# The reciprocal root of each norm: nine small VectorE operations where there were twelve

## The chip, the cores and the metric

The kernel runs on one core of one Trainium2 chip. The metric is device time in microseconds for one launch of the whole layer. A profiled execution also gives a trace of every instruction on the core's engines: TensorE (PE; its weight loads are listed apart as PEld), VectorE (DVE), ScalarE (ACT), GpSimd (POOL), and the queue from which transfers are issued (SP).

## The reference

One layer of a decoder on 1024 tokens of width 1024, in float32. Five kinds of norm run through it, and the change touches nothing else.

```python
def rms_norm(x, gain):
    xf = x.astype(jnp.float32)
    y = xf * lax.rsqrt(jnp.mean(xf * xf, axis=-1, keepdims=True) + EPS)
    return (y * gain.astype(jnp.float32)).astype(x.dtype)
...
    h = modulate(rms_norm(x, ffn1_norm[l]), sh1, sc1)
    x = x + 0.5 * g1[:, None, :] * swiglu(h, ...)              # width 2816
    h = modulate(rms_norm(x, mix_norm[l]), sh2, sc2)
    b_gate, c_gate, v, u = jnp.split(h @ w_in[l], ...)
    y_conv = short_conv_mixer(b_gate, c_gate, v, conv_w[l])
    y_ssm = s5_mixer(u, ...)                                  # diagonal state space, then a GLU
    y_mix = jnp.concatenate([rms_norm(y_conv, out_norm_conv[l]),
                             rms_norm(y_ssm, out_norm_ssm[l])], axis=-1)
    x = x + g2[:, None, :] * (y_mix @ w_out[l])
    h = modulate(rms_norm(x, ffn2_norm[l]), sh3, sc3)
    x = x + 0.5 * g3[:, None, :] * swiglu(h, ...)
return rms_norm(x, final_norm)
```

The nine vectors of shift, scale and gate come from a product of `silu(cond)` with a matrix of 1024 by 9216.

## The kernel before, in words

Activations lie transposed: the 128 partitions hold channels, the columns hold tokens. The 1024 tokens are two halves of 512 (`h` = 0, 1), the 1024 channels are eight tiles (`k`). Each large product is made of three matmuls with a high and a low part of both operands (`mm3`). ScalarE copies the high part of a weight tile and VectorE subtracts it for the low part; in the trace these are the rows that write `w`.

The stages follow each other: a prologue with the first norm (`p`); the first feed-forward block (names with `fa`, down projections `fad` and `fald`); the norm `n2`; the input projection (`u`, `c`, `v`, `b`) with the state space; the output norms `nA` (convolution) and `nB` (state space); the GLU (`gl`, whose input is split into `yg`); the output projection (`wo`); the norm `n3`; the second feed-forward block (`fb`, last products `fb10d`); the final norm in pieces, `n_0` for the first 512 tokens, `n_0` again for 256 and `n_256` for the last 256. A trailing `a` or `b` in a name is the half of the tokens. Products of the modulation matrix (`wm`), one for each 128 by 1024 piece of it, run on VectorE beside the main work, each after its own transfer into one of two buffers.

A norm goes like this (class `Sumsq`). ScalarE squares the tiles, VectorE or GpSimd add them, and small matmuls with a column of ones (`st`) put the sums of 128 tokens at a time into one column: 512 tokens become a block of 128 by 4. `roots` computes the reciprocal root of this block on VectorE, `wide` repeats each of the four columns 128 times (`rb`), and `spread` turns the result by matmuls with the identity, so that every partition holds the root of every token (`bc`). The consumers multiply by it.

The operations of `roots` write four small tiles: `v` (the mean plus epsilon), `i` (its bits as an integer), `a` and `y`; in the trace a norm's name, an `n` and that letter, as in `nBana`. Twelve norms of the program run `roots`: p, with 8 columns, two widenings and two `bc`; n2a, n2b, nAa, nAb, nBa, nBb, n3a, n3b and the first n_0, with 4; the second n_0 and n_256, with 2.

In the program, matmuls drive a counter (`Clock`): after each `mm3` it ticks, and `rstd` puts the sums, the root and the spreading some ticks later, so that matmuls of other work stand between them. Where a consumer needs the result at once, the counter is run forward (`ready`, `clock.until`), and nothing stands between. The order in which the instructions then stand on each engine is made by a planner of the framework, from dependencies, the order of the program and free buffers. Only in the prologue is the order of each engine fixed to that of the program:

```python
    InOrder.strict = True
    ...
    InOrder.strict = False
```

Almost every engine call goes through the helper `InOrder`, so the profile puts nearly all instructions at line 107, and groups are told apart by the tiles they write and read.

Of the kernel before, what the change touches and what calls it, by code (L numbers as in the profile page):

```python
# [15 lines left out]
I32 = mybir.dt.int32  # L16
AF = mybir.ActivationFunctionType
ALU = mybir.AluOpType
# [3 lines left out]
P = 128  # L22
# [30 lines left out]
RC2 = float(np.float32(np.round((TWO_PI - RC1) * 2.0**20) / 2.0**20))  # L53
RC3 = float(np.float32(TWO_PI - RC1 - RC2))
ROUND = 12582912.0
EXP_C = [1.9875691500e-4, 1.3981999507e-3, 8.3334519073e-3, 4.1665795894e-2, 1.6666665459e-1, 5.0000001201e-1]


# [173 lines left out]
def hymba_layer(ctx: ExitStack, tc, x_d, wm1_d, wmod_d, gu1_d, gs1_d, ds1_d, wl1_d, win_d, wout_d, glu_d, gu2_d, gs2_d, wd2_d, ds2_d, wl2_d, cols_d, cond_d, lam_d, bc_d, out_d):  # L232
    nc = tc.nc
    V, A, T, SP = (InOrder(tc, e) for e in (nc.vector, nc.scalar, nc.tensor, nc.sync))
# [33 lines left out]
    def t2k(name):  # L268
        return tmp.tile([P, HALF], F32, tag="t", name=name)
# [82 lines left out]
    class Sumsq:  # L352
# [28 lines left out]
        def rstd(self, width, use, wait=4, wait2=7):  # L381
            q = self.n // P

            def stats():
                st = sm([P, 4], self.name + "st")
                self.sums(st)
                y = roots(st, q, width, self.name)
                rb = wide(y, self.name)
                clock.after(wait2, lambda: use(spread(rb, self.name)))

            clock.after(wait, stats)

    def roots(st, q, width, nm):

        v, y, a = (const.tile([P, 8], F32, tag=f"n{i}", name=f"{nm}n{i}", bufs=1)[:, :q] for i in "vya")
        yi = const.tile([P, 8], I32, tag="ni", name=nm + "ni", bufs=1)[:, :q]
        V.tensor_scalar(out=v, in0=st[:, :q], scalar1=1.0 / width, scalar2=EPS, op0=ALU.mult, op1=ALU.add)
        V.tensor_scalar(out=yi, in0=v.bitcast(I32), scalar1=1, scalar2=None, op0=ALU.logical_shift_right)
        V.tensor_scalar(out=yi, in0=yi, scalar1=-1.0, scalar2=1597463007.0, op0=ALU.mult, op1=ALU.add)
        src = yi.bitcast(F32)  # L400
        for _ in range(3):
            V.tensor_tensor(out=a, in0=src, in1=src, op=ALU.mult)
            V.scalar_tensor_tensor(out=a, in0=a, scalar=-0.5, in1=v, op0=ALU.mult, op1=ALU.mult)
            V.scalar_tensor_tensor(out=y, in0=a, scalar=1.5, in1=src, op0=ALU.add, op1=ALU.mult)
            src = y
        return y

    def wide(y, nm):
        q = y.shape[1]
        rb = t2k(nm + "rb")[:, : q * P].rearrange("p (a b) -> p a b", a=q)  # L410
        V.tensor_copy(rb, y.unsqueeze(2).to_broadcast([P, q, P]))
        return rb

    def spread(rb, nm):
# [358 lines left out]
    for h in range(2):  # L773
# [7 lines left out]
        q = sqs[0]  # L781
        V.tensor_tensor(out=q[:, :HALF], in0=q[:, :HALF], in1=q[:, HALF:], op=ALU.add)
        for i in range(4):
            c = 4 * h + i
            T.matmul(st[:, c : c + 1], lhsT=q[:, i * P : (i + 1) * P], rhs=one[:], start=True, stop=True)
    y = roots(st, 8, D, "p")
    rbs = [wide(y[:, 4 * h : 4 * h + 4], f"p{h}") for h in range(2)]
    ws.open(ringp, 2)
    w4 = ws.take(2)
# [94 lines left out]
    def ssm_base(sb1):  # L884
# [9 lines left out]
        def exp_(dst, src):  # L894
            k, r, z, s = w[0], w[1], w[2], w[3]
            V.tensor_scalar(out=s, in0=src, scalar1=-87.0, scalar2=88.0, op0=ALU.max, op1=ALU.min)
            V.tensor_scalar(out=k, in0=s, scalar1=1.0 / math.log(2.0), scalar2=ROUND, op0=ALU.mult, op1=ALU.add)
            V.tensor_scalar(out=k, in0=k, scalar1=ROUND, scalar2=None, op0=ALU.subtract)
            V.scalar_tensor_tensor(out=r, in0=k, scalar=-0.693359375, in1=s, op0=ALU.mult, op1=ALU.add)
            V.scalar_tensor_tensor(out=r, in0=k, scalar=2.12194440e-4, in1=r, op0=ALU.mult, op1=ALU.add)  # L900
            V.tensor_scalar(out=z, in0=r, scalar1=EXP_C[0], scalar2=None, op0=ALU.mult)
            for c in EXP_C[1:]:
                V.scalar_tensor_tensor(out=z, in0=z, scalar=c, in1=r, op0=ALU.add, op1=ALU.mult)
            V.tensor_tensor(out=z, in0=z, in1=r, op=ALU.mult)
            V.scalar_tensor_tensor(out=z, in0=z, scalar=1.0, in1=r, op0=ALU.add, op1=ALU.add)
            ki = sb1.tile([P, G], I32, tag="ki", name="ki", bufs=2)
            V.tensor_scalar(out=ki[:], in0=k, scalar1=127.0, scalar2=8388608.0, op0=ALU.add, op1=ALU.mult)
            V.tensor_tensor(out=dst, in0=z, in1=ki[:].bitcast(F32), op=ALU.mult)
# [7 lines left out]
        exp_(r, ar)  # L916
        V.tensor_scalar(out=w[0], in0=th, scalar1=1.0 / TWO_PI, scalar2=ROUND, op0=ALU.mult, op1=ALU.add)
        V.tensor_scalar(out=w[0], in0=w[0], scalar1=ROUND, scalar2=None, op0=ALU.subtract)
        for c in (RC1, RC2, RC3):
# [747 lines left out]
```

## Time and profile before

| | |
|---|---|
| median of three runs | 1745.43 us (1743.46 to 1748.77) |
| profiled execution: time | 1741.48 us |
| its span, first to last instruction | 1739.7 us |
| TensorE busy | 1672.0 us, 96% |
| VectorE busy | 1291.1 us, 74%, 2261 instructions |
| ScalarE busy | 573.3 us, 33% |
| GpSimd busy | 352.8 us, 20% |
| mean granted TensorE clock | 0.992 |

Busy time is summed over stages with different limits. A row of a timeline gives the start, the duration, the engine, the operation, the tiles written and read, the shapes and the number of instructions merged in the row; in brackets stands how long the engine was idle before it and which instruction ended that. A row of the windows gives a stretch, its length, the busy time with the number of instructions, the granted clock, the share of the transfer engines and GB/s. A row of the groups gives the number of instructions, their busy time in us, the mean of one in ns and the idle time before them.

### The profile page before, as it was taken

Reading aid. Unit: us, or ns where it says so; the run is one execution under the profiler, and the core shown is the slowest. Engines: PE = TensorE matmul, PEld = TensorE weight load, DVE = VectorE, ACT = ScalarE, POOL = GpSimd, SP = SyncE. Lnnn points to the kernel's source line nnn. Section 1 sums busy time; section 2 is a strip of 40 time slices with the busy share of each in tenths; the row PEclk is TensorE's granted clock in tenths of the full one; section 3 lists DMA queues with packets and bytes.
Section 4 is the critical chain, followed back from the end, with each engine's and each line's share of the span. In section 5 each row is a group of like instructions: output and inputs, shape, how many; then the busy total and the mean of one; then the engine's idle time right before and its main releaser. Section 6 shows DMA issues by size and latency. Waiting matters only on the chain.

```text
span 1739.7 us, 20839 instructions
## 1 busy us (share of the span) xinstructions
PE 1672.0 (96%) x7532; PEld 1375.3 (79%) x7532; DVE 1291.1 (74%) x2261; ACT 573.3 (33%) x944; POOL 352.8 (20%) x241
## 2 busy tenths in 40 slices
PE   4999999999999999999999999999999999999996
PEld 3788888787887878887877778778888888888886
DVE  7999999998656787644657977967776666576656
ACT  4233334344332222331114424424444433322221
POOL 0000132222422221100000021123223323333211
PEclk9999999999999999999999999999999999999998
DMA  8245644555787877234654450114344334659212
GB/s 322 84 145 197 220 158 167 179 201 173 286 307 275 321 259 270 73 86 147 209 152 152 134 181 25 49 49 157 144 175 166 133 138 152 249 235 379 104 49 97
DMA packets 101338, 304.56 MB, mean 175 GB/s; under 512 B 19313, under 2 KB 34929, under 8 KB 90098
## 3 DMA queue, kind: packets, MB, share of 16 engines
q1 hardware_dynamic: 101234, 303.22, 49.0%
q8 instruction: 59, 0.97, 0.2%
q14 instruction: 45, 0.37, 0.1%
HBM read 212.47 MB, written 86.51 MB: 172 GB/s over the span
## 4 chain that ended last, share of the span: by engine, by line
PE 64%; DVE 8%; DMA 3%; issue 1%; ACT 0%; POOL 0%; SPq 0%; DVEq 0%; ACTq 0%; POOLq 0%
PE wo L107 4%; PE fald L107 3%; PE fb10d L107 2%; PE u L107 2%; PE fbd_1B L107 2%; PE fbd_0B L107 2%; PE fad_1B L107 2%; DVE w L107 2%; PE fad_0B L107 2%; PE b L107 2%; DMA swz<-si 1%; DVE x L107 1%; PE fb0g L107 1%; PE fbd_1C L107 1%; PE fbd_0C L107 1%; PE fbd_1A L107 1%
## 5 line engine op out<-in xcount | busy, mean ns | idle before, releaser
L107 ACT CAST w<-raw 128x512 fp32r<-128x512 f32 (+1 forms) x358 | 235.9, 689 | 459.1 <-issue 70.1
L107 DVE TENSOR_TENSOR w<-raw,w 128x512 fp32r<-128x512 f32 (+1 forms) x358 | 300.9, 860 | 100.8 <-ACT w L107 99.9
L164 POOL TENSOR_TENSOR sums<-raw 128x512 f32<-128x512 f32 x50 | 73.8, 1476 | 452.9 <-DMA raw<-in_gs 271.0
L173 POOL TENSOR_TENSOR raw<-sums,raw 128x512 f32<-128x512 f32 x50 | 78.4, 1568 | 367.3 <-DVE w L107 353.7
L107 DVE CUSTOM_DVE_ANT_0 wm<-wm,cact 128x1024 f32<-128x1024 f32 x56 | 77.7, 1396 | 22.6 <-DMA wm<-in_wmod 22.6
L175 POOL TENSOR_TENSOR raw<-raw 128x512 f32<-128x512 f32 x50 | 77.1, 1542 | 79.1 <-DVE w L107 79.1
L165 POOL TENSOR_TENSOR raw<-raw 128x512 f32<-128x512 f32 x50 | 77.3, 1547 | 3.1
L366 POOL TENSOR_TENSOR n3aq<-n3aq,n3aq 128x512 f32<-128x512 f32 x5 | 7.4, 1474 | 279.1 <-ACT n3aq L107 278.9
L107 DVE TENSOR_TENSOR w<-sums,w 128x512 fp32r<-128x512 f32 x50 | 56.7, 1147 | 5.4 <-ACT w L107 4.8
L107 PE MATMUL p<-h,w 128*128 128x512 f32 x192 | 49.6, 421 | 8.1 <-DVE h L107 5.3
L107 PEld LDWEIGHTS p<-h,w 128*128 128x128 f32 x192 | 39.1, 205 | 18.6 <-DVE h L107 6.5
L107 PE MATMUL wo<-oa,w 128*128 128x512 f32 x192 | 45.6, 392 | 2.1 <-ACT w L107 1.4
L107 PE MATMUL v<-h,w 128*128 128x512 f32 x192 | 46.8, 395 | 0.0
L107 PE MATMUL c<-h,w 128*128 128x512 f32 x192 | 46.6, 394 | 0.0
L107 PE MATMUL b<-h,w 128*128 128x512 f32 x192 | 45.6, 393 | 0.0
L107 PE MATMUL wo<-ob,w 128*128 128x512 f32 x192 | 45.5, 392 | 0.0
L107 PE MATMUL u<-h,w 128*128 128x512 f32 x192 | 44.7, 391 | 0.2 <-DVE h L107 0.2
L107 PEld LDWEIGHTS wo<-oa,w 128*128 128x128 f32 x192 | 35.8, 188 | 10.2 <-ACT w L107 1.8
L107 PEld LDWEIGHTS u<-h,w 128*128 128x128 f32 x192 | 35.7, 188 | 8.3 <-DVE h L107 0.6
L107 PEld LDWEIGHTS wo<-ob,w 128*128 128x128 f32 x192 | 35.7, 188 | 7.7 <-DVE ob L107 0.4
L107 PEld LDWEIGHTS b<-h,w 128*128 128x128 f32 x192 | 35.5, 188 | 7.2
L107 PEld LDWEIGHTS c<-h,w 128*128 128x128 f32 x192 | 35.4, 188 | 7.0
(1566 smaller groups left out, 4028.4 us busy)
## 6 DMA issues: line engine op xcount, KB each, us to landing
raw<-in_gs SPq DMA_DIRECT2D x34, 1024.0 KB, 5.5
wm<-in_wmod SPq DMA_DIRECT2D x56, 512.0 KB, 5.8
raw<-in_ds SPq DMA_DIRECT2D x16, 1024.0 KB, 6.8
raw<-in_gu SPq DMA_DIRECT2D x10, 1024.0 KB, 7.1
mw<-in_wm SPq DMA_DIRECT2D x8, 1024.0 KB, 12.4
x<-in_x SPq DMA_DIRECT2D x16, 512.0 KB, 8.3
raw<-in_win SPq DMA_DIRECT2D x8, 1024.0 KB, 5.6
raw<-in_wl SPq DMA_DIRECT2D x5, 1024.0 KB, 6.6
```

The lines of the kernel that those rows point to most:

```text
L107: r = getattr(self.engine, name)(*args, **kw)
L164: self.G.tensor_tensor(out=f, in0=r[2], in1=r[1], op=ALU.subtract)
L165: self.G.tensor_tensor(out=r[1], in0=r[1], in1=r[0], op=ALU.subtract)
L173: self.G.tensor_tensor(out=r, in0=s["t3"], in1=r, op=ALU.add)
L175: self.G.tensor_tensor(out=r, in0=self.chunk(j, 3), in1=r, op=ALU.subtract)
L366: nc.gpsimd.tensor_tensor(out=a, in0=a, in1=sq[:, :n], op=ALU.add)
```

## The change

The seed of the root is the usual one from the bits of the float: half of the bits, subtracted from a constant. Before, one operation shifts the bits and a second negates and adds. After, one operation multiplies the integer by −0.5 and adds a constant. Then, before, three Newton steps of three operations each. After, one step with tuned constants in three operations, and a step of third order in four. That step ends with a factor of 0.375, which is left out of the root; the widening, a copy before, multiplies by it. In all, nine operations in place of twelve, and no other edit.

```diff
+ROOT_BITS, ROOT_A, ROOT_B = 1595932665.0, 0.703952253, 2.38924456
...
         V.tensor_scalar(out=v, in0=st[:, :q], scalar1=1.0 / width, scalar2=EPS, op0=ALU.mult, op1=ALU.add)
-        V.tensor_scalar(out=yi, in0=v.bitcast(I32), scalar1=1, scalar2=None, op0=ALU.logical_shift_right)
-        V.tensor_scalar(out=yi, in0=yi, scalar1=-1.0, scalar2=1597463007.0, op0=ALU.mult, op1=ALU.add)
+        V.tensor_scalar(out=yi, in0=v.bitcast(I32), scalar1=-0.5, scalar2=ROOT_BITS, op0=ALU.mult, op1=ALU.add)
         src = yi.bitcast(F32)
-        for _ in range(3):
-            V.tensor_tensor(out=a, in0=src, in1=src, op=ALU.mult)
-            V.scalar_tensor_tensor(out=a, in0=a, scalar=-0.5, in1=v, op0=ALU.mult, op1=ALU.mult)
-            V.scalar_tensor_tensor(out=y, in0=a, scalar=1.5, in1=src, op0=ALU.add, op1=ALU.mult)
-            src = y
+        V.scalar_tensor_tensor(out=a, in0=src, scalar=-ROOT_A, in1=src, op0=ALU.mult, op1=ALU.mult)
+        V.tensor_tensor(out=a, in0=a, in1=v, op=ALU.mult)
+        V.scalar_tensor_tensor(out=y, in0=a, scalar=ROOT_A * ROOT_B, in1=src, op0=ALU.add, op1=ALU.mult)
+        V.tensor_tensor(out=a, in0=y, in1=y, op=ALU.mult)
+        V.tensor_tensor(out=a, in0=a, in1=v, op=ALU.mult)
+        V.scalar_tensor_tensor(out=a, in0=a, scalar=-10.0 / 3.0, in1=a, op0=ALU.add, op1=ALU.mult)
+        V.scalar_tensor_tensor(out=y, in0=a, scalar=5.0, in1=y, op0=ALU.add, op1=ALU.mult)
         return y
...
-        V.tensor_copy(rb, y.unsqueeze(2).to_broadcast([P, q, P]))
+        V.tensor_scalar(out=rb, in0=y.unsqueeze(2).to_broadcast([P, q, P]), scalar1=0.375, scalar2=None, op0=ALU.mult)
```

## Prediction

> **What bounds the kernel now.** I read the page first, for the busiest engine and for the chain that ended last.
>
> ```profile
> span 1739.7 us, 20839 instructions
> PE 1672.0 (96%) x7532; PEld 1375.3 (79%) x7532; DVE 1291.1 (74%) x2261; ACT 573.3 (33%) x944; POOL 352.8 (20%) x241
> PE 64%; DVE 8%; DMA 3%; issue 1%; ACT 0%; POOL 0%; SPq 0%; DVEq 0%; ACTq 0%; POOLq 0%
> ```
>
> TensorE is busy for 96% of the span, and the chain lies on it for 64%; VectorE (DVE) holds only 8% of the chain. A shorter norm on DVE can therefore bring time only where TensorE stands still for it. So the second view is the waits of TensorE: who waited for whom, microseconds in total, times, longest.
>
> ```profile
> PE n_256bc L107 <- DVE n_256rb L107: 4.2, 1, 4.2
> PE nBabc L107 <- DVE nBarb L107: 3.9, 1, 3.9
> PE p0bc L107 <- DVE p0rb L107: 3.0, 1, 3.0
> PE n_0bc L107 <- DVE n_0rb L107: 2.5, 1, 2.5
> PE gl L107 <- DVE yg L107: 1.9, 1, 1.9
> PE nAbbc L107 <- DVE nAbrb L107: 1.7, 1, 1.7
> ```
>
> Each norm ends in `rb`, the widened root, and `bc`, eight (or four) matmuls that spread it. Twelve norms run `roots`, and only five of them (p, nAb, nBa, the second n_0, n_256) stand here; `gl`, behind `yg`, is a neighbour of nAb. 17.2 us in all is the most that norms could ever give back.
>
> **The change part by part.** *The three operations removed.* `roots` issues twelve small operations before and nine after: 36 fewer in twelve norms. The price of one is read where they run back to back, in the prologue (timeline of VectorE, start and duration; then TensorE).
>
> ```profile
> 22.11 0.17 DVE L107 TENSOR_SCALAR pnv<-p_st 128x8 f32<-128x8 f32 x1 [1.96 <-PE p_st L107]
> 24.53 0.43 DVE L107 COPY p0rb<-pny 128x512 f32<-128x512 f32 x1
> 25.10 2.05 PE L107 MATMUL p0bc<-ident,p0rb 128*128 128x128 f32 x8 [3.03 <-DVE p0rb L107]
> ```
>
> Twelve operations lie between 22.11 and 24.53: 2.42/12 = 0.202 us each, start to start, of which 0.17 is the operation. Three fewer are 0.61 us. The new operations are of the removed kinds at the same width, and I price them alike; the fused bit step takes the place of a multiply-add on the same integers.
>
> [...]
>
> *The prologue.* There the order of issue is tied down, TensorE waits 3.0 us for `p0rb`, and everything after starts from it: −0.61 us, which the rest of the kernel inherits.
>
> *Norms that TensorE does not wait for.* In the main part the spreading matmuls come some 20 matmuls after the sums, and those cover the root:
>
> ```profile
> 719.03 0.43 DVE L107 COPY n2arb<-n2any 128x512 f32<-128x512 f32 x1
> 720.36 1.05 PE L107 MATMUL n2abc<-ident,n2arb 128*128 128x128 f32 x8
> ```
>
> `n2arb` ends 0.9 us before TensorE comes to it. The bc of n2b, n3a, n3b, nAa, nBb and the first n_0 are not in the list of waits either: 0 for these seven. Were the matmuls in front gone, their roots would show in full (0.6 us of saving each); nothing in the change touches them.
>
> *nAb.* Here two waits must be kept apart.
>
> ```profile
> 940.88 0.16 DVE L107 TENSOR_SCALAR nAbnv<-nAbst 128x4 f32<-128x4 f32 x1 [1.15 <-PE nAbst L107]
> 943.06 0.69 DVE L107 TENSOR_TENSOR yg<-yb,yg 128x512 fp32r<-128x512 f32 x1 [0.23 <-issue]
> 943.86 0.16 DVE L107 SCALAR_TENSOR_TENSOR nAbny<-nAbna,nAbny 128x4 f32<-128x4 f32 x1
> 952.64 0.42 DVE L107 COPY nAbrb<-nAbny 128x512 f32<-128x512 f32 x1
> ```
>
> The root is done at 944.0 and the widening runs at 952.64: the wait of 1.7 us at `nAbbc` is not the root's, 0 from it. But `yg`, for which `gl` waits, stands behind ten of the root's operations. If it goes behind seven, −0.6; if the planner puts nine and the widening ahead of it, +0.2. I take −0.4.
>
> *nBa.*
>
> ```profile
> 967.45 1.23 DVE L107 TENSOR_TENSOR w<-raw,w 128x1024 fp32r<-128x1024 f32 x1 [0.86 <-ACT w L107]
> 971.06 1.22 DVE L107 CUSTOM_DVE_ANT_0 wm<-wm,cact 128x1024 f32<-128x1024 f32 x1
> 972.21 0.16 DVE L107 SCALAR_TENSOR_TENSOR nBany<-nBana,nBany 128x4 f32<-128x4 f32 x1
> 972.97 2.04 PE L107 MATMUL nBabc<-ident,nBarb 128*128 128x128 f32 x8 [3.92 <-DVE nBarb L107]
> ```
>
> Between `w`, which the root does not hold up, and `nBarb` lie the nine operations of the three old steps, and large ones of other work. Seven take the place of the nine; the third removed operation stood ahead of `w` and brings nothing. So −0.4, at 0.2 each. If the two stood inside other work they would be worth 0.08 each, −0.16; that is the near bound, and the far one is a rival below.
>
> *The end.* After the last weights the span is a chain on VectorE.
>
> ```profile
> 1720.64 0.16 DVE L107 TENSOR_SCALAR n_0ni<-n_0nv 128x2 int32<-128x2 int32 x1
> 1720.73 0.48 DVE L107 SCALAR_TENSOR_TENSOR x<-fb10d,gate,x 128x256 f32<-128x256 f32 x1
> 1725.74 0.29 DVE L107 COPY n_0rb<-n_0ny 128x256 f32<-128x256 f32 x1
> 1730.51 0.16 DVE L107 TENSOR_TENSOR n_256na<-n_256ny 128x2 f32<-128x2 f32 x1
> 1731.69 0.29 DVE L107 COPY n_256rb<-n_256ny 128x256 f32<-128x256 f32 x1
> 1733.30 3.22 DVE L107 SCALAR_TENSOR_TENSOR x<-x,cols,n_256bc 128x256 f32<-128x256 f32 x8 [1.32 <-PE n_256bc L107]
> ```
>
> The second n_0 runs in the gaps of output work: an operation between two large ones costs 0.09 (1720.64 to 1720.73), a free-standing one 0.2. Three fewer are −0.26 to −0.6; VectorE is full there and most stand in gaps, so −0.3. In n_256 the last six operations run alone (1.18/6 = 0.197 each) and the output multiplies follow: −0.59.
>
> *The widening.* A copy of 128x512 becomes a multiply by 0.375. The trace has no such multiply at 512 columns.
>
> ```profile
> L107 DVE TENSOR_SCALAR w<-w 128x32 f32<-128x32 f32 x18 | 3.2, 180 | 0.5
> L107 DVE TENSOR_SCALAR tab<-pw 64x288 f32<-64x288 f32 x4 | 1.2, 300 | 0.0
> L107 DVE TENSOR_TENSOR X<-X,st 128x512 f32<-128x512 f32 x8 | 5.5, 691 | 0.2
> ```
>
> The two TENSOR_SCALAR rows give 120 ns for 256 columns, so 405 ns at 512, against 0.43 us for the copy: nothing, or 0.02 gained. The other bound is a two-input operation, 691 ns: +0.26 in each of the two p widenings and nBa, +0.13 in each of the two half-width ones, about +1.1 us in all. I take 0, by the rows of its own kind.
>
> *Sum:* −0.61 −0.4 −0.4 −0.3 −0.59 = −2.3 us. The change adds no wait and no transfer, and moves no step past a queue. The profiled execution took 1741.48 us (its span is 1739.7) and would take 1739.2. It lies 4 us under the median of the three runs, 1745.43, which becomes 1743.1, or −0.13%. Less than 0.3%, 5.2 us, a measurement of this kernel can hardly tell from no change.
>
> **The rivals.** All rest on one thing that the trace shows: in the code a root's operations follow each other, but on VectorE other work stands between them. A planner orders the engines, and three fewer operations can change its order anywhere.
>
> *Faster, the waits shrink further.* If the second `wm` of nBa (1.15 us from 971.06 to 972.21) falls behind the widening, and `nAbrb` moves forward to its root, that is −1.15 and −1.7. Then TensorE's clock joins in.
>
> ```profile
> 972.90:974.70 1.80, 1.73 (x9) 0.50 0.64 180
> 953.10:954.10 1.00, 0.99 (x9) 1.00 0.85 324
> 953.11 1.16 PE L107 MATMUL nAbbc<-ident,nAbrb 128*128 128x128 f32 x8 [1.74 <-DVE nAbrb L107]
> 974.67 3.77 PE L107 MATMUL gl<-yg,w 128*128 128x512 f32 x12
> 936.62 2.88 PE L107 MATMUL gl<-yg,w 128*128 128x512 f32 x12
> ```
>
> After the wait of 3.92 us the granted clock was 0.50; after 1.74 us it was 1.00. The same eight matmuls took 2.04 against 1.16, and the twelve behind them 3.77 against 2.88: the drop cost 0.88 + 0.89 = 1.8 us. Together: 2.3 + 1.15 + 1.7 + 1.8 = 7.0, 1738.5 us. For it: the planner has moved such work through every root in sight, and `nAbrb` stands 8.6 us behind its root. Against it: three steps have to fall together.
>
> *The clock alone.* The wait falls from 3.9 to 3.5 us and the clock stays up: −2.3 − 1.8 = −4.1, 1741.3 us. The trace says only that the limit lies between 1.74 and 3.92 us, so 3.5 is more likely beyond it than not. [...]
>
> *It does less than it says.* Other work closes the gaps at nAb, nBa and n_0; the prologue and n_256 remain: −1.2, 1744.2 us.
>
> *Slower: a `wm` ahead of a weight.* `wm` are the side products that wait for their own loads.
>
> ```profile
> 1021.06 3.44 DVE L107 TENSOR_TENSOR w<-raw,w 128x1024 fp32r<-128x1024 f32 x2
> 1024.43 2.31 DVE L107 CUSTOM_DVE_ANT_0 wm<-wm,cact 128x1024 f32<-128x1024 f32 x1
> 1026.66 1.22 DVE L107 CUSTOM_DVE_ANT_0 wm<-wm,cact 128x1024 f32<-128x1024 f32 x1
> 1031.61 1.22 DVE L107 CUSTOM_DVE_ANT_0 wm<-wm,cact 128x1024 f32<-128x1024 f32 x1 [3.72 <-DMA wm<-in_wmod]
> ```
>
> If the planner lets the weights at 1021.06 slip behind these three, TensorE, which needs them at once, waits until 1032.8 minus 1024.4 = 8.4 us longer: 1745.43 − 2.3 + 8.4 = 1751.5 us. Two of them alone cost 3.4 and leave the time about as it was. It decides from the third on. For it: loads are late there (3.72 us). Against it: the planner held the weights first here.
>
> **How the numbers follow.** The forecast as summed 0.46 (its own range 1742.6 to 1745.1, all lower and all upper bounds of its terms added); the clock alone 0.16; less than it says 0.10; faster together 0.19; slower 0.09. Within 0.3% are the first three, 0.72; faster 0.19; slower 0.09. The range runs from just under the faster rival, 1737.0, to 1748.5, where two thirds of the slower one's price are paid; what is left out is the full slower case and a little of the faster.
>
> **What would show it.** Nine operations in each root of the changed profile, 36 fewer on VectorE and about 6 us less busy time; `p0bc` 0.6 us earlier; the wait of `n_256bc` 0.6 shorter, 3.6 us; `nBabc` waiting 3.5; the widening at 0.41 to 0.43 us; the granted clock at `nBabc`. It is wrong if VectorE's order differs around `wm`, `nAbrb` or the weights, or if the widening comes near 0.69 us.

## The result, and the profile after

The median fell from 1744.75 to 1741.66 us (17 runs of each; 1742.04 to 1748.77 before, 1735.41 to 1744.90 after). The ratio, worked out from all the runs, is 0.9974, with a 95% interval of 0.9966 to 0.9982: 4.5 us less, between 3.1 and 5.9; the two medians alone differ by 3.1. The forecast was 2.3 us less.

The profiled execution of the changed kernel took 1742.49 us, 1.0 more than the one of before. Single executions differ by the granted clock (0.988 to 0.993 in the 17 of the changed kernel, with 1735.41 to 1744.90 us), so that two spans alone decide nothing here. The cores view of the changed kernel gives the span and the mean granted clock (1739.7 us and 0.992 before).

```profile
core 0: 1740.3 us, clock 0.989
```

The clock's shortfall from 1, times the span, is an estimate of the most time given up: 1739.7 × 0.008 = 13.9 us and 1740.3 × 0.011 = 19.1 us. At the same clock the changed kernel's execution would by that be 0.6 − 5.2 = 4.6 us shorter, with about 1.2 us of rounding: the size of the ratio. What the change did must be read from its places, then. The page of the changed kernel:

```profile
PE 1674.2 (96%) x7532; PEld 1377.1 (79%) x7532; DVE 1287.5 (74%) x2225; ACT 573.8 (33%) x944; POOL 352.2 (20%) x241
```

VectorE has 36 operations fewer, as forecast, and 3.6 us less of busy time, not the 6 forecast, so 0.10 us for each: many stand between large operations and overlap them (in the trace of before, one of 0.16 us at 1720.64 and a large one 0.09 us later). One constant more in the file puts the helper at line 108. TensorE's waits for norms, of the changed kernel (total, times, longest):

```profile
PE n_256bc L108 <- DVE n_256rb L108: 3.8, 1, 3.8
PE p0bc L108 <- DVE p0rb L108: 2.4, 1, 2.4
PE nBabc L108 <- DVE nBarb L108: 2.3, 1, 2.3
PE n_0bc L108 <- DVE n_0rb L108: 1.9, 1, 1.9
PE nAbbc L108 <- DVE nAbrb L108: 1.7, 1, 1.7
PE gl L108 <- DVE yg L108: 1.7, 1, 1.7
PE nBbbc L108 <- DVE nBbrb L108: 0.7, 1, 0.7
```

Five fell: p from 3.0 to 2.4, the second n_0 from 2.5 to 1.9, n_256 from 4.2 to 3.8, `gl` behind `yg` from 1.9 to 1.7, and nBa from 3.9 to 2.3. The last is far more than three operations can give. A small new one stands at nBb. The sum of all these is 14.5, from 17.2.

The prologue, on VectorE and then TensorE of the changed kernel:

```profile
22.12 0.17 DVE L108 TENSOR_SCALAR pnv<-p_st 128x8 f32<-128x8 f32 x1 [1.96 <-PE p_st L108]
23.93 0.43 DVE L108 TENSOR_SCALAR p0rb<-pny 128x512 f32<-128x512 f32 x1
```

```profile
24.50 2.05 PE L108 MATMUL p0bc<-ident,p0rb 128*128 128x128 f32 x8 [2.42 <-DVE p0rb L108]
```

Nine operations in 1.81 us, 0.201 each, and `p0bc` at 24.50 instead of 25.10. The widening, now a multiply, lasts 0.43 us, as the copy did.

nBa: first two rows of VectorE and one of TensorE from the trace of before, then VectorE and TensorE of the changed kernel:

```profile
968.66 1.22 DVE L107 CUSTOM_DVE_ANT_0 wm<-wm,cact 128x1024 f32<-128x1024 f32 x1
972.40 0.43 DVE L107 COPY nBarb<-nBany 128x512 f32<-128x512 f32 x1
978.28 1.98 PE L107 MATMUL wo<-oa,w 128*128 128x512 f32 x8
```

```profile
969.07 1.23 DVE L108 TENSOR_TENSOR w<-raw,w 128x1024 fp32r<-128x1024 f32 x1 [1.00 <-ACT w L108]
970.29 1.22 DVE L108 CUSTOM_DVE_ANT_0 wm<-wm,cact 128x1024 f32<-128x1024 f32 x1
972.41 0.43 DVE L108 TENSOR_SCALAR nBarb<-nBany 128x512 f32<-128x512 f32 x1
972.75 1.22 DVE L108 CUSTOM_DVE_ANT_0 wm<-wm,cact 128x1024 f32<-128x1024 f32 x1
```

```profile
972.98 1.13 PE L108 MATMUL nBabc<-ident,nBarb 128*128 128x128 f32 x8 [2.30 <-DVE nBarb L108]
973.87 4.59 PE L108 MATMUL gl<-yg,w 128*128 128x512 f32 x12
978.29 1.98 PE L108 MATMUL wo<-oa,w 128*128 128x512 f32 x8
```

Before, two `wm` (at 968.66 and 971.06) stood between `w` and `nBarb`; now the second runs at 972.75, behind the widening. From the start of `w` to that of `nBarb` it is 3.34 us instead of 4.95: 1.15 of the 1.61 are the `wm`, and 0.46 the operations. The planner moved it, not the diff. Behind the wait nothing was gained: from `nBabc` to the next `wo` both traces take 5.31 us.

nAb, the late weights and the end, on VectorE of the changed kernel:

```profile
942.90 0.16 DVE L108 TENSOR_SCALAR nAbnv<-nAbst 128x4 f32<-128x4 f32 x1 [1.15 <-PE nAbst L108]
944.48 0.16 DVE L108 SCALAR_TENSOR_TENSOR nAbny<-nAbna,nAbny 128x4 f32<-128x4 f32 x1
944.88 1.29 DVE L108 TENSOR_TENSOR yg<-yb,yg 128x512 fp32r<-128x512 f32 x2 [0.24 <-issue]
954.46 0.42 DVE L108 TENSOR_SCALAR nAbrb<-nAbny 128x512 f32<-128x512 f32 x1
...
1021.04 3.45 DVE L108 TENSOR_TENSOR w<-raw,w 128x1024 fp32r<-128x1024 f32 x2
...
1726.95 0.29 DVE L108 TENSOR_SCALAR n_0rb<-n_0ny 128x256 f32<-128x256 f32 x1
1729.23 0.15 DVE L108 TENSOR_SCALAR n_256nv<-n_256st 128x2 f32<-128x2 f32 x1
1732.32 0.30 DVE L108 TENSOR_SCALAR n_256rb<-n_256ny 128x256 f32<-128x256 f32 x1
```

`yg` starts 1.98 us behind `nAbnv`, where it was 2.18: it now stands behind nine operations, not ten. `nAbrb` still comes ten microseconds after its root. The late weights still start at 1021. n_256 takes 3.09 us from `nv` to `rb`.

By stages of TensorE (from the first matmul of one tile to that of the next) the changed execution is shorter by 0.6 us up to `p0bc`, 0.2 from the sums of nAb to `nAbbc`, 1.8 from `nAbbc` to `nBabc`, 0.2 from the sums of the first n_0 to its `n_0bc`, 0.7 from there to the second `n_0bc` and 0.6 from there to `n_256bc`: 4.1 us in all. One stage of a norm goes the other way: from `nBabc` to the sums of n3 it takes 76.26 us instead of 75.52, 0.7 longer, and in it stands the new wait of 0.7 us at `nBbbc`. By an estimate the rest is mostly the clock: ahead of the end, it stood at 0.50 for eight stretches of 3.41 us here and for five before, and three of them at half the clock are up to 5.1 us of work.

### The profile page after: what moved, and what is told of

Read it like the earlier page. It is cut to its first block, busy times and chain, and to the rows that moved or that the text cites. A ratio compares the mean times of both kernels' runs of the same rounds, so it can differ in the third digit from the quotient of the medians.

```text
span 1740.3 us, 20803 instructions
## 1 busy us (share of the span) xinstructions
PE 1674.2 (96%) x7532; PEld 1377.1 (79%) x7532; DVE 1287.5 (74%) x2225; ACT 573.8 (33%) x944; POOL 352.2 (20%) x241
## 4 chain that ended last, share of the span: by engine, by line
PE 63%; DVE 8%; DMA 4%; issue 1%; SPq 1%; POOL 1%; ACT 1%; DVEq 0%; ACTq 0%; POOLq 0%
PE fald L108 3%; PE wo L108 2%; PE fb10d L108 2%; PE u L108 2%; PE fbd_1B L108 2%; PE fbd_0B L108 2%; PE fad_0B L108 2%; PE fad_1B L108 2%; PE b L108 1%; DVE w L108 1%; DVE x L108 1%; DMA swz<-si 1%; PE v L108 1%; PE fb0g L108 1%; PE fbd_1C L108 1%; PE fbd_0C L108 1%
```

## The experiments

A root has 12 operations before and 9 in the changed kernel. Each set was timed against the kernel before on its own chip; a ratio is to that kernel and carries its 95% interval.

**1. The count put back.** Three idle operations behind the new root.

```diff
+        for _ in range(3):
+            V.tensor_scalar(out=y, in0=y, scalar1=1.0, scalar2=None, op0=ALU.mult)
         return y
```

> The changed kernel with three further small operations at the end of each root (y times 1.0), so twelve operations as before, with the new widening. Theory A (the gain is the number of operations, where TensorE waits for a root): the gain goes, ratio to before 1.000, nBabc waits about 3.9 us again. Theory B (the kind of the operations, or the widening as a multiply): the gain stays, ratio 0.997.

1746.09 us, ratio 1.0004 (0.9994 to 1.0013). Its order on every engine is that of before, and so are its waits (3.9 at nBa, 4.1 at n_256, 3.0 at p, 2.5 at n_0). Theory A came out: the gain hangs on the number of operations, not on their kind. The order came back together with the number; experiment 8 separates the two.

**2. The widening alone.** The old root, widened by a multiply.

```diff
-        V.tensor_copy(rb, y.unsqueeze(2).to_broadcast([P, q, P]))
+        V.tensor_scalar(out=rb, in0=y.unsqueeze(2).to_broadcast([P, q, P]), scalar1=1.0, scalar2=None, op0=ALU.mult)
```

> The kernel before with one edit, the widening as a multiply by 1.0 where it was a copy. Theory A: 0.42 to 0.43 us for 512 columns, ratio to before 1.000. Theory B (the multiply is what brings the gain): ratio 0.997.

1746.5 us, ratio 1.0013 (1.0001 to 1.0026). The interval leaves out 1 by a hair, but the timeline of VectorE in that kernel shows no cost:

```profile
24.51 0.43 DVE L107 TENSOR_SCALAR p0rb<-pny 128x512 f32<-128x512 f32 x1
```

That is the duration of the copy, and the order and the waits are those of before. What differs is the mean granted clock of its executions, 0.9878 against 0.9889, worth up to 1.9 us by the table at the end of this part. That the multiply lowers the clock isn't shown; experiment 1 has it too, at 0.9888.

**3. and 4. More steps, fewer steps.** The changed kernel without its second step (five operations; the root has the accuracy of one step), and the kernel before with six Newton steps (21 operations).

```diff
# five
-        V.tensor_tensor(out=a, in0=y, in1=y, op=ALU.mult)
-        V.tensor_tensor(out=a, in0=a, in1=v, op=ALU.mult)
-        V.scalar_tensor_tensor(out=a, in0=a, scalar=-10.0 / 3.0, in1=a, op0=ALU.add, op1=ALU.mult)
-        V.scalar_tensor_tensor(out=y, in0=a, scalar=5.0, in1=y, op0=ALU.add, op1=ALU.mult)
...
# six steps
-        for _ in range(3):
+        for _ in range(6):
```

> The changed kernel without its third-order step: five operations in each root, the widening multiplies by 1.0 (the root is left at the accuracy of one step). Theory A, linear at the forecast's 0.77 us for each operation (2.3 us for three): seven fewer than before are 5.4 us, ratio 0.9969. Theory C (the gain is mostly a step, the clock at nBabc that no longer falls, 1.8 us once): 5.4 + 1.8 = 7.2 us, ratio 0.9959, and hardly less clock lost than in the changed kernel. Theory B: 0.997 as the changed kernel.

> The kernel before with six Newton steps in place of three, 21 operations in each root, the widening a copy. Theory A: nine more operations at 0.77 us are 6.9 us, and the covers of n2a and nAa (0.9 us each) and of n2b (none) run out by 0.9, 0.9 and 1.8 us: 10.5 us, ratio 1.0060. Theory D (TensorE's waits are set by other work, and roots fit in beside it): under 4 us, ratio below 1.0023.

1735.0 us, ratio 0.9944 (0.9927 to 0.9961), and 1758.35 us, ratio 1.0081 (1.0064 to 1.0099). Both moved further than any of the expectations: for five, 0.9959 lies just inside the interval and 0.9969 outside it; for 21, 1.0060 was the most expected. Per operation that is 1.4 us in the one and 1.6 in the other, against 0.77 in my sum. With 21, covered norms come into sight, though not those I had named: n3b waits 1.6 us and nBb 1.2, but n2a only 0.3, nAa 0.2, and n2b not at all. Two of TensorE's waits of that kernel:

```profile
PE nBabc L107 <- DVE nBarb L107: 6.7, 1, 6.7
...
PE n3bbc L107 <- DVE n3brb L107: 1.6, 1, 1.6
```

**5., 6. and 7. The new root in some norms only.** In nAb and nBa; in the seven that TensorE does not wait for; in p, the second n_0 and n_256. The others keep the old root, and are widened with a factor of 1.

```diff
+        if nm in ("nAb", "nBa"):        # or the seven, or the ends
             ...                         # nine operations
+        else:
+            ...                         # the old twelve
...
-        V.tensor_scalar(out=rb, ..., scalar1=0.375, scalar2=None, op0=ALU.mult)
+        V.tensor_scalar(out=rb, ..., scalar1=0.375 if nm in ("nAb", "nBa") else 1.0, scalar2=None, op0=ALU.mult)
```

> The nine-operation root in nAb and nBa alone, the old root in the other ten norms (all widenings are multiplies). By the forecast's terms: -0.4 -0.4 = -0.8 us, ratio 0.9995. If the excess of the gain over the forecast sits here (in the changed trace the widening of nBa stands ahead of a side product of 1.15 us): the stretch from nAbbc to nBabc 1.7 us shorter, in all -2.0 us, ratio 0.9988.

> The nine-operation root in the seven norms that the forecast counted as nothing (n2a, n2b, n3a, n3b, nAa, nBb, the first n_0), the old root in the rest. By the forecast: 0, ratio 1.000. If the excess sits here (covers that do not hold on every execution, or freed VectorE time): -2.2 us, ratio 0.9987.

> The nine-operation root in p, the second n_0 and n_256 alone, the old root in the rest. By the forecast: -0.61 -0.3 -0.59 = -1.5 us, ratio 0.9991; p0bc 0.6 us earlier, the stretches from the second n_0's sums to the end 0.9 us shorter. The rival that the place does not matter and each norm brings a twelfth: a quarter of 4.5 us, -1.1 us, which its time alone will not tell apart; the stretches will.

| new root in | us | ratio | in us |
|---|---|---|---|
| nAb, nBa | 1742.74 | 0.9977 (0.9968 to 0.9987) | −4.0 |
| the seven covered | 1744.82 | 0.9994 (0.9983 to 1.0005) | −1.0 |
| p, second n_0, n_256 | 1743.50 | 0.9982 (0.9972 to 0.9992) | −3.1 |

Covered norms are worth nothing that can be measured. The ends give more than the 1.9 us that their waits lose (p 2.4, n_0 1.9, n_256 3.5) and than the 1.5 expected, but both lie within the interval. The two norms of the middle give 4.0, with the same move of the `wm` as in the changed kernel; the 2.0 us that I had expected at most lie just outside the interval. The three add to −8.1, more than the −4.5 of the whole; each carries ±1.7 us, so that the gap of 3.6 stands against an uncertainty of about 3.4. That is the edge of what the intervals allow, and whether the parts really add up stays open.

**8. The order alone.** The old root everywhere; an order without a wait ties that one side product behind nBa's widening.

```diff
+        held_back[nm] = V.tensor_copy(rb, y.unsqueeze(2).to_broadcast([P, q, P]))
...
+        if (n, d) == (SC3, 6):
+            info = mybir.DependencyInfo(mybir.DependencyClass.NoSync, mybir.DependencyReason.DATA)
+            tc.add_manual_dep(got.ins, held_back["nBa"].ins.name, info, reason="behind the root of nBa")
```

> The old root of twelve operations in all norms; the only edit is an order tie that puts one side product (the second wm of nBa) behind nBa's widening, where the changed kernel has it. Theory (in nBa the order of that wm was worth more than the removed operations): the wait at nBabc falls from 3.9 to about 2.7 us, the stretch from nAbbc to nBabc is 1.1 to 1.2 us shorter, and the time falls by 1.2 us, up to 2.8 where the granted clock also survives the wait (ratio to the kernel before 0.9993 down to 0.9984). Rival (the gain at nBa comes from the root's operations and the wm costs as much behind the widening): wait and stretch shorter by less than 0.3 us in sum with what follows, time 1.000.

1745.76 us, ratio 0.9993 (0.9982 to 1.0005). The timelines of VectorE and of TensorE in that kernel:

```profile
971.86 1.23 DVE L107 TENSOR_TENSOR w<-raw,w 128x1024 fp32r<-128x1024 f32 x1 [0.99 <-ACT w L107]
975.79 0.43 DVE L107 COPY nBarb<-nBany 128x512 f32<-128x512 f32 x1
976.13 1.22 DVE L107 CUSTOM_DVE_ANT_0 wm<-wm,cact 128x1024 f32<-128x1024 f32 x1
```

```profile
976.37 2.04 PE L107 MATMUL nBabc<-ident,nBarb 128*128 128x128 f32 x8 [2.90 <-DVE nBarb L107]
978.06 5.02 PE L107 MATMUL gl<-yg,w 128*128 128x512 f32 x12
982.92 5.81 PE L107 MATMUL wo<-oa,w 128*128 128x512 f32 x24
```

The wait falls from 3.92 to 2.90 us, and from `nAbbc` to `nBabc` it is 1.2 us less: the order alone makes two thirds of the changed kernel's 1.8 there, and the rest is the operations'. But the time is not measurably lower, and by the sum of the wait and what follows the rival's number came out: from `nBabc` to `wo` it took 6.55 us, 1.24 more than in the trace of before. Not the `wm` took that back, though; the same matmuls ran slower, and the windows of that trace show at what clock (the third column from the end), here and in the next 3.41 us too:

```profile
975.61:979.02 3.41, 2.65 (x10) 2.54 (x11) 3.38 (x7) 1.02 (x2) 0.00 (x0) 0.50 0.48 161
```

The drop held for 6.83 us where it held for 3.42 before. The edit did not move that one product alone, either: further on the planner put two more `wm` later, one of them behind the widening of nBb, whose wait is 0.9 us here, and changed the order of some `wo` matmuls. Those moves come behind nBa, so its stage is a clean test of the order, and the whole time is not.

**9., 10. and 11. The clock in nBa's wait.** First, small matmuls that read each state of the root, to keep TensorE at work while it is computed (in the changed kernel):

```diff
+        def busy(x):
+            if nm == 'nBa':
+                for _ in range(3):
+                    T.matmul(st[:, :q], lhsT=ident[:], rhs=x, start=True, stop=True)
+        busy(y)        # and behind each of the four operations that follow
```

> The changed kernel, with fifteen small matmuls (identity by a 128x4 state of the root, results unused) between the steps of nBa's root, so that TensorE is not idle for the whole wait there. Theory (a wait without matmuls of about 2 us or more sometimes loses the clock, and that costs 1.6 us): granted clock at nBabc 1.00, the stretch from nBabc to the first wo 3.7 us where the changed kernel's trace has 5.3, time about 0.5 to 1.6 us under the changed kernel's, ratio to the kernel before 0.9971 to 0.9965. Rival (the clock's share of the gain is not made in this wait): stretch 5.3 again or no change of time, ratio 0.9974; if the small matmuls hold up nBabc, slower than that by up to 1 us.

1745.74 us, ratio 0.9996 (0.9984 to 1.0008): the gain of the change is gone. The timelines of VectorE and TensorE, and then two windows (the granted clock is the third column from the end):

```profile
978.14 0.16 DVE L107 TENSOR_TENSOR nBana<-nBana,nBanv 128x4 f32<-128x4 f32 x1 [1.40 <-PE nBast L107]
979.23 0.16 DVE L107 SCALAR_TENSOR_TENSOR nBana<-nBana 128x4 f32<-128x4 f32 x1 [0.92 <-PE nBast L107]
```

```profile
981.22 2.05 PE L107 MATMUL nBabc<-ident,nBarb 128*128 128x128 f32 x8 [0.27 <-DVE nBarb L107]
```

```profile
976.60:980.90 4.30, 3.79 (x30) 3.57 (x30) 1.95 (x7) 0.00 (x0) 0.00 (x0) 1.00 0.35 122
981.00:984.40 3.40, 3.18 (x12) 2.92 (x13) 3.40 (x7) 1.23 (x2) 0.00 (x0) 0.51 0.51 154
```

The root writes `a` and `y` again, and two of its steps waited for the matmuls that read the state before: 1.40 and 0.92 us. Besides, the second `wm` stood ahead of the widening again (at 979.51 us, with `nBarb` at 980.65), which takes back the 1.15 us that the changed kernel had gained by it. In TensorE's waits only 0.3 us stands at `nBabc`, but the path to it was longer: from `w` to `nBarb` 6.62 us instead of 3.34. And the clock fell to 0.51 all the same, after 4.3 us in which TensorE counts as 88% busy with matmuls of four columns. Neither the theory nor the rival came out: this kernel did not save the clock, and cannot tell whether saving it pays.

Second, matmuls of 512 columns that need nothing of the root, into the bank of `nBabc` ahead of it, where they are overwritten: eight in the changed kernel, ten in experiment 8's. All other engines keep the order of their base.

```diff
         bc = ps(nm + "bc")
+        for fill in idle.pop(nm, ()):
+            T.matmul(bc[:], lhsT=fill[:, :P], rhs=fill, start=True, stop=True)
...
+    idle["nBa"] = [actG[1][0][0]] * 8
     glu(1)
```

> The changed kernel with eight matmuls of 512 columns (results overwritten) put into the bank of nBabc ahead of it, in nBa only; they need nothing of the root and fill about 1.9 of the 2.3 us that TensorE stands still there. The order of everything else is that of the changed kernel. Theory (what is lost at nBa beside the wait is the clock, which falls when TensorE stands still): wait at nBabc 0.3 to 0.5 us, granted clock 1.00 through the twelve gl matmuls behind it, stretch from nBabc to the next wo 3.7 us where the changed kernel's trace had 5.3; time under the changed kernel's by as much of 1.6 us as its executions lose there, ratio to the kernel before 0.9974 to 0.9965. Rival (the clock follows a clock of its own, whatever TensorE does in that wait): stretch 5.3 us in this trace too, ratio 0.9974; the matmuls put ahead of the last three gl can make it up to 1 us slower.

> The old root with the side product tied behind nBa's widening, and ten matmuls of 512 columns in the wait of 2.9 us at nBabc. Theory (clock falls because TensorE stands still): the stretch from nBabc to the next wo falls from 6.5 us, with the clock lost, to about 3.7 us at a clock of 1.00, and the time lies 1.6 us under that of the tie alone, ratio to the kernel before about 0.9984. Rival (no relation to idling): the clock is lost as before, ratio 0.9993.

1739.02 us, ratio 0.9970 (0.9959 to 0.9982), and 1742.95 us, ratio 0.9985 (0.9976 to 0.9993). TensorE of the first:

```profile
968.86 1.98 PE L107 MATMUL nBabc<-yg 128*128 128x512 f32 x8
971.90 1.16 PE L107 MATMUL nBabc<-ident,nBarb 128*128 128x128 f32 x8 [0.39 <-DVE nBarb L107]
972.82 3.00 PE L107 MATMUL gl<-yg,w 128*128 128x512 f32 x12
975.65 5.81 PE L107 MATMUL wo<-oa,w 128*128 128x512 f32 x24
```

From `nBabc` to `wo` it is 3.75 us, where the changed kernel's trace has 5.31; in the second kernel 3.74 us, where its base has 6.55. `nBabc` takes 1.16 us in the first, as `nAbbc` did at a clock of 1.00 in the trace of before. Both traces came out as the theory said and not as the rival did: what experiment 8 lost behind its wait was the clock. In the times, the second lies 0.8 of a thousandth (1.4 us) under its base and the first 0.4 (0.7 us) under the changed kernel, as expected in sign, but the intervals overlap: the price of the clock is shown in the traces, not by the medians.

**12. A version that beats both.** One step of fourth order from the seed, seven operations in a root, the leading factor in the widening.

```diff
...                                     # another constant in the seed
+        V.tensor_tensor(out=y, in0=src, in1=src, op=ALU.mult)
+        V.tensor_tensor(out=y, in0=y, in1=v, op=ALU.mult)
+        V.scalar_tensor_tensor(out=a, in0=y, scalar=-3.85391955, in1=y, op0=ALU.add, op1=ALU.mult)
+        V.scalar_tensor_tensor(out=a, in0=a, scalar=5.8901439, in1=y, op0=ALU.add, op1=ALU.mult)
+        V.scalar_tensor_tensor(out=y, in0=a, scalar=-5.39785411, in1=src, op0=ALU.add, op1=ALU.mult)
...                                     # the seven operations of the changed kernel go; another factor in the widening
```

> A version meant to beat both: one step of fourth order from the seed (relative error of the root 8e-7 over the range, by calculation), seven operations in each root, the leading factor in the widening. At the slope that the kernels with 5, 9, 12 and 21 operations show (1.2 us for each at equal clock, 1.5 with the clock's share), two fewer than the changed kernel: -2.4 to -3.0 us against it, ratio to before 0.9958. If the gain sits in steps already taken (order at nBa): about -1.5 us against it, ratio 0.9966.

1737.65 us, ratio 0.9946 (0.9934 to 0.9959): under the kernel before and, the intervals being apart, under the changed one. Of the two numbers expected, 0.9958 lies in the interval and 0.9966 does not. Its waits at p and the second n_0 are 2.0 and 1.3 us, and the longest:

```profile
PE n_256bc L107 <- DVE n_256rb L107: 3.1, 1, 3.1
PE nBabc L107 <- DVE nBarb L107: 1.9, 1, 1.9
```

**All together.** The norms' waits are those of the `bc` matmuls and of `gl` behind `yg`, summed over the trace, against 17.2 us in the trace of before. The clock is the mean over the timed executions, against that of the kernel before in the same set; the difference is turned into time with 1745 us.

| kernel | operations | change by the ratio, us | norms' waits, us | clock, us |
|---|---|---|---|---|
| five | 5 | −9.8 | −8.5 | −4.0 (0.9912 against 0.9889) |
| seven | 7 | −9.4 | −5.3 | −5.8 (0.9914, 0.9881) |
| nAb and nBa | 9, 12 | −4.0 | −1.0 | −3.0 (0.9898, 0.9881) |
| the ends | 9, 12 | −3.1 | −1.9 | −1.6 (0.9890, 0.9881) |
| the covered | 9, 12 | −1.0 | +0.2 | −0.2 (0.9882, 0.9881) |
| order alone | 12 | −1.2 | −0.2 | −0.9 (0.9887, 0.9882) |
| count put back | 12 | +0.7 | −0.1 | +0.2 (0.9888, 0.9889) |
| widening alone | 12 | +2.3 | −0.1 | +1.9 (0.9878, 0.9889) |
| six steps | 21 | +14.1 | +12.4 | +6.8 (0.9850, 0.9889) |

The difference of two clock means has a standard error of 0.4 to 0.9 thousandths, 0.8 to 1.5 us. Within that, the two columns add up to the change in every row but the first and the last, where they overshoot by 2.7 and 5.1. But the clock column books every microsecond of the shortfall as lost, and that is its upper end: over the 224 executions of all these kernels, each compared with the others of its own kernel and set, a mean clock lower by 0.001 goes with 0.76 us more (±0.15), and in the 17 of the changed kernel alone with 1.3, against 1.7 in the column. Why it is less than the column was not shown. So the sum of the columns doesn't prove the split. Of the 2.3 us of the widening, the clock of its executions is 0.8 to 1.9, and that is within the noise. The kernels of experiments 9 to 11 are left out, because their added matmuls stand in the waits. My reading is that a shorter wait gives its length and, in part of the executions, one drop of the clock less; shown is that only at nBa (from `nBabc` to `wo` 5.31 us with the drop, 3.75 without).

## Why the prediction was right, point by point

The forecast stood within 0.3% with a chance of 0.72, and 0.26% it was; 1743.1 us lies 1.4 above the median of after, of which 0.7 is the base: the kernel before came out at 1744.75, not 1745.43. Part of that is luck. The forecast as summed had a range of its own, 1742.6 to 1745.1, and 1741.66 lies below it; the number is nearest to the rival of the clock alone, 1741.3, whose mechanism did not come (the wait was 2.3 us, not 3.5, and the clock fell). And by one of my own signs, another order around `wm`, the mechanism was wrong at nBa. The reason was right: operations count only where TensorE waits (experiments 1, 6 and 7), at 0.20 us each where they run alone. The sum of the terms, −2.3, was half of what was measured. It also held that the change adds no wait, and nBb got one of 0.7 us. Term by term, by the traces:

- **p, −0.61: right.** Wait 3.03 to 2.42 us, `p0bc` 0.60 earlier.
- **yg, −0.4: too much.** It went behind nine operations instead of ten, so 0.2.
- **nBa, −0.4: the step that failed.** The operations brought 0.46, in the place I gave; but I took the order as it stood, and the planner put the second `wm` behind the widening. That is the step priced at 1.15 us under the faster rival, and the order alone moved the stage by 1.2. The rival needed two more steps: `nAbrb` did not move, and the clock fell in the trace at this place all the same. So one of its three came true, and its chance of 0.19 was for all three together; the single steps should have stood as cases of their own.
- **Second n_0, −0.3: too little.** I counted most operations as standing in gaps. But the last three before `n_0rb` ran alone in the trace of before, from 1725.15 (below) to 1725.74, and these are the ones that went: 0.6.

```profile
1725.15 0.16 DVE L107 TENSOR_TENSOR n_0na<-n_0ny 128x2 f32<-128x2 f32 x1
```

- **n_256, −0.59: right.** From `nv` to `rb` 3.67 us before, 3.09 after. Its wait fell only from 4.2 to 3.8, not to the 3.6 I had said.
- **Covered norms, 0: right within the noise.** The first n_0 showed 0.2 in the trace, nBb lost 0.7 by its new wait, and the set of seven has an interval that holds 0.
- **The widening, 0: right.** 0.43 us; the upper bound, the row of 691 ns for a two-input operation, was the wrong kind.
- **Left out of the sum: the clock.** I treated it as one event at nBa, to be kept or lost, and thought that a wait of 3.5 us might keep it. The last part shows one wait of 2.3 us that lost it and one that kept it, and how long TensorE stood still ahead of the drops; by an estimate from those numbers, 3.5 us would hardly have kept it. Over all executions it is an average: 0.9904 for the changed kernel, 0.9881 to 0.9889 for the kernel before in the four sets of the experiments. That is 1.2 to 4.0 us, by the two prices above, and between sets measured apart, so only a rough share; the terms of the trace, −4.1, and the clock overlap at nBa.

The slower rival did not come: some side products between 975 and 1041 us moved, but the weights at 1021 kept ahead of them.

## What to carry to other kernels

Here a shorter chain of small operations paid only where the matrix engine stood still for its result (−3.1 us at the three ends, −1.0 with an interval that holds 0 at the seven covered norms); read those places from the waits, and in each count the operations that run alone just ahead of the result: at the second n_0 these were the three that went, for 0.6 us. If a planner orders the engines, look at the large side work between the small operations: at nBa one piece of it was worth 1.15 us and the operations 0.46, and an edit that did not name it moved it. Compare the two orders before the times. And when two profiled executions differ by less than the clock takes (1.0 us here, against up to 5.2 by the clock), compare waits and stages, not spans; a stage that gains can be followed by one that gives some of it back, as the one from `nBabc` did here with 0.7 us.

## What the runs showed of the hardware

**A wait of 2.3 us lost the clock, 1.3 us behind its end.** In the changed kernel's trace TensorE stood still from 970.68 to 972.98, came back at full clock, and lost it 1.3 us into the work. The windows around it (the clock is the third column from the end):

```profile
970.68:972.98 2.30, 0.00 (x1) 0.03 (x1) 2.13 (x9) 0.00 (x0) 0.00 (x0) 1.00 0.19 55
972.98:974.28 1.30, 1.30 (x10) 1.26 (x11) 1.30 (x3) 0.00 (x0) 0.00 (x0) 1.00 0.87 309
974.28:977.70 3.42, 3.42 (x10) 2.64 (x9) 3.42 (x7) 1.23 (x2) 0.00 (x0) 0.50 0.62 181
```

The drop lasts 3.42 us at 0.50, so up to 1.7 us of work. Before, it lasted as long, with TensorE idle 3.9 us ahead of it:

```profile
969.00:972.88 3.88, 0.06 (x1) 0.00 (x0) 3.64 (x14) 0.00 (x0) 0.00 (x0) 1.00 0.45 151
972.88:976.30 3.42, 3.33 (x12) 3.07 (x13) 3.42 (x6) 1.81 (x3) 0.00 (x0) 0.50 0.64 180
```

With the same wait of 2.30 us, the kernel with the new root in nAb and nBa kept the clock; waits of 1.9 and 1.5 us (seven and five operations) kept it; 2.9 us (order alone) and the 3.9 us of five traces lost it.

**The drops of one trace start whole steps of 3.41 us apart, and followed the steps with the most idling.** The records of the granted clock in the traces of before and after give every drop to 0.50. The step is worked out from them: (974.288 − 32.209)/276 = 3.4133 us, and the starts lie on whole steps to 0.003 us. The last column is the share of the step ahead of the drop in which TensorE stood still, matmuls of one column (a norm's sums) and of up to four counted as standing still.

| trace | start of the drop, us | steps behind the first | length, us | stood still |
|---|---|---|---|---|
| before | 44.455 | 0 | 6.827 | |
| before | 546.214 | 147 | 3.413 | 62% |
| before | 972.880 | 272 | 3.413 | 100% |
| before | 1133.307 | 319 | 3.413 | 55% |
| before | 1727.226 | 493 | to the end | |
| after | 32.209 | 0 | 6.827 | |
| after | 45.863 | 4 | 3.413 | |
| after | 400.849 | 108 | 3.413 | 78% |
| after | 547.622 | 151 | 3.413 | 54% |
| after | 742.182 | 208 | 3.413 | 56% |
| after | 974.288 | 276 | 3.413 | 62% |
| after | 1141.541 | 325 | 3.413 | 56% |
| after | 1728.633 | 497 | to the end | |

The records of the other 12 traces gave whole steps of the same length. Where the steps lie against the kernel differs: the first drops of these two are 44.455 − 32.209 = 12.246 us apart, 3.59 steps. And equal waits are cut by the steps in different ways. The step ahead of the drop in the changed kernel, and two steps over the equal wait of the kernel that kept the clock (nAb and nBa), by the windows:

```profile
970.87:974.28 3.41, 1.30 (x10) 1.29 (x11) 3.24 (x11) 0.00 (x0) 0.00 (x0) 1.00 0.43 147
```

```profile
969.83:973.24 3.41, 1.62 (x8) 1.00 (x6) 3.23 (x10) 1.15 (x2) 0.00 (x0) 1.00 0.39 145
973.24:976.65 3.41, 2.90 (x17) 2.59 (x18) 3.29 (x6) 1.24 (x2) 0.00 (x0) 1.00 0.63 199
```

The first wait lies almost whole in one step, in which TensorE stood still for 2.11 us, 62%. The second is cut: 1.79 us (52%) fall into one step and 0.51 into the next. Between 50 and 1715 us (ahead of that the records of the clock are not complete) the traces of before and after hold 966 steps at full clock. Counted as in the table, a drop followed the eight with 54% idle or more, 54.3% the least, and none of the 958 others, 53.4% the most. All 14 traces hold 6763 such steps, and in them a drop followed none of the 6683 with less than 51% idle, all 43 with 56% or more, and 19 of the 37 between. So less than 1.74 us of standing still within one step never went ahead of a drop in these traces, and 1.91 us or more always did; what decides between the two was not shown. An estimate from these numbers, with the limit taken at 1.8 us: if the steps fall anywhere with equal chance, a wait of 3.9 us always loses the clock and one of 2.3 us about six times in ten, so that the changed kernel saves 0.4 × 1.7 = 0.7 us at nBa on average, which its own trace does not show.

**Matmuls of few columns did not keep the clock here.** Matmuls of four columns filled 88% of 4.3 us in experiment 9 and the clock went, to 0.51 in the 3.4 us behind; with eight of 512 columns in 1.98 us it stayed (experiment 10: `nBabc` in 1.16 us behind them). The eight one-column matmuls of n2b's sums seem to count as little: in six traces a drop followed a step around them with only 29% idle in the profile, but 56% when they are counted as standing still; in the changed kernel's trace that is the step from 738.77 us, ahead of the drop at 742.18. What in such matmuls makes the difference was not tried.
